# A hybrid decoder layer on one core: the scores of all four pairs of heads in one block, and the last two pairs taken out one gate tile sooner

## The chip, the core and the metric

The kernel runs on one core of a Trainium2 chip. Its engines are TensorE (PE in the profile, with its weight loads PEld), VectorE (DVE), ScalarE (ACT), GpSimd (POOL) and SyncE (SP), which here only issues transfers. Each engine works through its own queue in order and waits for the others by semaphores. The metric is device time in microseconds (us) of one execution, as the median of several runs.

## The reference, cut to what matters

One layer over 256 tokens of width 1024, all in float32: a norm, an input projection `w_in` into q, k, v (8 heads of 64), a pooling input and two gates of 1024 features; causal attention (all 256 tokens lie in one block, so block selection adds nothing) beside a causal multi-scale pooling; both branches projected, gated, summed and projected out; then a gated FFN with a depthwise convolution.

```python
q = apply_partial_rotary(rmsnorm(heads(q), q_norm_g), pos)
k = apply_partial_rotary(rmsnorm(heads(k), k_norm_g), pos)
attn = moba_attention(q, k, heads(v))          # softmax(q k^T / 8, causal) v, per head
pooled = multiscale_pool_mixer(u_pool, w_pool, pool_scale)
gates = sigmoid(gate_logits + b_gate)
mixed = gates[0] * (attn @ w_branch_attn) + gates[1] * (pooled @ w_branch_pool)
x = x + mixed @ w_out
```

## The kernel before, in words

**Numbers and weights.** Each float32 operand is split into a rounded part (`high`, on ACT, tiles `hi_*`) and the rest (`low`, on DVE, tiles `lo_*`); a product takes three matmuls (`mm3`: hi·hi, hi·lo, lo·hi). Weights come in blocks of 1 MB, numbered in the order in which they are used: 15 and 16 are the last two blocks of the gates (`raw_g`), 17 and 18 `w_branch_pool` (`raw_bp`), 19 and 20 `w_branch_attn` (`raw_ba`), 21 to 24 `w_out` (`raw_o`). There are four raw buffers: block c is loaded once block c-4 has been split (`loads`, called from `next_low`). `ahead()` puts the next pieces of splitting into the queues of ACT and DVE between other work.

**Stages around the change.** After q, k, v and the pooling input come 16 gate tiles of 24 matmuls each (`ps_g0` to `ps_g15`, loop over `n`). Between them lie the scores of the attention. The eight heads make four pairs; a pair's two heads use the upper and the lower 64 rows of TensorE. The product of the small projections of pooling, `pool_maps`, comes ahead of gate tile 12. Then come eight tiles of the pool branch (`ps_bp0` to `ps_bp7`); in the midst of them, after tile 4, TensorE multiplies the softmax weights with the values (`values`, `ps_o`). Then come eight tiles of the attention branch (`ps_ba0` to `ps_ba7`), whose moving operand is `heads`, and then `w_out` and the FFN.

**One pair's way.** Scores on TensorE (10 instructions); on DVE the causal mask is added and the row's maximum taken (`sm`, `mx`); on ACT the exponentials, with their sums (`rsum`); on DVE a transposition of 32x32 blocks; on SP a store to memory (`spill`, `home_w`) and four loads (`fill`) that finish the transposition; on TensorE the values. The reciprocals of the sums take a way of their own after the last pair: DVE (`yr`), a store `home_sums`, and two loads into `RS`. `rounded` multiplies the values with `RS` on DVE and rounds on ACT, and `rests` makes the low part of `heads` on DVE.

**What sets the order.** The order is written out: instructions stand in each queue as the Python code calls them, and a last loop ties each engine to it. `later(n, fn)` puts a step n gate tiles (later: n pairs of branch tiles) off. While `paused[0]` is set, `loads` issues nothing of itself; from then on single blocks are let through by `loads(1)` in `turn_weights` (after the last pair's store) and in `fill_late` (after the last fills), until `fill_late` lifts the pause.

**PSUM and SBUF.** `mm` has four single banks, which all tiles of 256 columns use in turn; `ps2` has two pairs of banks. In the kernel before, each pair's scores take one pair of banks, so two pairs are done ahead of gate tile 6 and two ahead of gate tile 10, each time followed by their masks. In SBUF `big` is a tag with two buffers (first q and k, then `sm0` and `y0`), and "qk" and "at" are the places of the split q and k.

Of the kernel before, what the change touches and what calls it, by code (L numbers as in the profile page):

```python
# [7 lines left out]
F32 = mybir.dt.float32  # L8
F32R = mybir.dt.float32r
AF = mybir.ActivationFunctionType  # L10
ALU = mybir.AluOpType
AX = mybir.AxisListType

P = 128
S = 256
NT = S // P
D = 1024
KD = D // P
H = 8
DH = 64  # L20
# [34 lines left out]
FFN_AHEAD = 6  # L55
MAPS = 6
VALUES = 4
GATES = (4, 5, 0, 1, 2, 6, 7, 3)
PLAIN = (4, 5, 6, 7, 8, 9)
HALVED = 2  # L60
# [10 lines left out]
def hybrid_layer_kernel(ctx: ExitStack, tc: tile.TileContext, xq_d, xtok_d, par_d, wkv_d, wpg_d,  # L71
                        wpool_d, wba_d, wbp_d, wout_d, wup_d, wdn_d, out_d):
    nc = tc.nc
# [5 lines left out]
    act = ctx.enter_context(tc.tile_pool(name="act", bufs=1))  # L79
# [3 lines left out]
    ps2 = pairs.enter_context(tc.tile_pool(name="ps2", bufs=2, space=bass.MemoryType.PSUM))  # L83
    tmp = mixer.enter_context(tc.tile_pool(name="tmp", bufs=2))

    def bank(name):
        return mm.tile([P, 512], F32, tag="mm", name=name)
# [57 lines left out]
    for c, (name, src) in enumerate(order):  # L145
        n = CH if name == "q" else src.shape[-1]
# [3 lines left out]
    for c in range(len(order) - 1):  # L150
        if order[c][0] == "dn" and order[c + 1][0] == "up":
            i = next(n for n, p in enumerate(pieces) if p[0] == c)
            pieces[i + 1:i + 4] = [*pieces[i + 2:i + 4], pieces[i + 1]]
    pieces[0:HALVED] = [(0, slice(256 * i, 256 * (i + 1)), i == 0, False) for i in range(2 * HALVED)]
    at = [0, 0]
# [31 lines left out]
    paused = [False]  # L187
# [67 lines left out]
    mask = const.tile([P, 2, P], F32, name="mask")  # L255
# [25 lines left out]
    rows = dram.tile([1, S], F32, name="rows")  # L281
# [61 lines left out]
    def big(name):  # L343
        return tmp.tile([P, 2 * 2 * 3 * P], F32, tag="big", bufs=2, name=name)
# [135 lines left out]
    for b in range(2):  # L480
        w = chunk("p")
        for c in range(2):
            ps = feature_tile(w, c, f"u{b}{c}")
# [15 lines left out]
    qp = act.tile([P, 2, KA, S], F32R, tag="qk", name="qp")  # L499
    kp = act.tile([P, 2, KA, S], F32R, tag="at", name="kp")  # L500
# [18 lines left out]
    def gate(n):  # L519
        return gates[:, n // 2, n % 2, :]  # L520
# [3 lines left out]
    TOK = (slice(0, P), slice(P, 3 * P))  # L524

    whole = mask.rearrange("p a b -> p (a b)")

    turned = []

    def scores(hps):  # L530
        if not turned:
            sms, ys = big("sm0"), big("y0")
            turned.append(ys)
        else:
            sms = turned.pop()
            ys = act.tile([P, 2 * 2 * 3 * P], F32, tag="qk", name="y2")
        pss = []
        for hp in hps:
            pss.append(ps2.tile([P, 2, 512], F32, tag="ps2", name=f"ps_s{hp}"))
            for t, part, keys in ((1, 1, 0), (1, 0, 0), (1, 0, 1), (0, 0, None), (0, 1, 0)):  # L540
                for j in range(2):
                    rows = slice(j * DH, (j + 1) * DH)
                    out = pss[-1][:, j, TOK[t]]
                    if keys is None:
                        out = pss[-1][:, j, :].rearrange("p (a b) -> p a b", b=P)[:, 0:4:3, :]
                    nc.tensor.matmul(out, qp[rows, part, hp, t * P:(t + 1) * P],
                                     kp[rows, :, hp, 0:P] if keys is None else kp[rows, keys, hp, 0:(t + 1) * P],
                                     start=t == part == 1, stop=(t, part, keys) in ((1, 0, 1), (0, 1, 0)),
                                     skip_group_check=True)
        for i, (hp, ps) in enumerate(zip(hps, pss)):  # L550
            on = slice(i * 6 * P, (i + 1) * 6 * P)
            sm = sms[:, on].rearrange("p (j c) -> p j c", j=2)
            mx = tmp.tile([P, 2, 2], F32, tag="mx", name=f"mx{hp}")
            nc.vector.tensor_tensor(sm[:, :, TOK[0]], ps[:, :, 3 * P:4 * P],
                                    mask[:, 1:2, :].to_broadcast([P, 2, P]), ALU.add)
            for j in range(2):
                for t in (1, 0):
                    nc.vector.tensor_tensor_reduce(sm[:, j, TOK[t]], ps[:, j, TOK[t]],
                                                   whole if t else sm[:, j, TOK[0]], 1.0, LOWEST,
                                                   ALU.add, ALU.max, mx[:, t, j:j + 1])  # L560
            nc.vector.scalar_tensor_tensor(mx, mx, -1.0, qs[:, :, 2 * hp:2 * hp + 2], ALU.mult, ALU.mult)
            if i == 0:
                exponentials(hp, sm, mx, ys[:, on], sms[:, on])
            else:
                behind.append((exponentials, hp, sm, mx, ys[:, on], sms[:, on]))
# [16 lines left out]
    RS = []  # L582
# [22 lines left out]
    def fill_late(far):  # L605

        for weights in late:
            fill_weights(*weights)
        loads(1)
        RS.append(act.tile([P, H // 2 * NT * P], F32, tag="qk", name="RS"))  # L610
        for j in range(2):
            src = far.rearrange("(a i) r -> a (i r)", a=4)[None, :, j * S:(j + 1) * S].to_broadcast([DH, 4, S])
            nc.sync.dma_start(out=RS[0][j * DH:(j + 1) * DH, :].rearrange("p (a c) -> p a c", a=4), in_=src)
        paused[0] = False
        loads()

# [10 lines left out]
        return po  # L627

    def weighed(hp):
        return RS[0].rearrange("p (a h t r) -> p h a t r", a=4, t=NT, r=32)[:, hp]  # L630

    def natural(hp):
        return weighed(hp).rearrange("p a t r -> p t a r")
# [43 lines left out]
    for n in range(2 * KD):  # L677
        if n == 1:
            for _ in range(2):
                next_high()  # L680
            for _ in range(2):
                next_low()
        if n in (2, 3):
            part_high("q" if n == 2 else "k")
        if n in (6, 10):
            scores((0, 1) if n == 6 else (2, 3))
            paused[0] = n == 10
        if n == 2 * MAPS:
            pool_maps()
            ahead()  # L690
        b, c = n // 2, n % 2
        if c == 0:
            w = chunk("g")
        ps = feature_tile(w, c, f"g{n}")
        tick()
        ahead(AHEAD if n % 2 else 0)
        for fn, *args in behind + held:
            fn(*args)
        behind.clear()
        held.clear()  # L700
        f = 2 * GATES[b] + c
        if n in PLAIN:
            nc.scalar.activation(gate(f), ps[:, 0:S], AF.Copy)
            plain.append(f)
        else:
            nc.vector.tensor_tensor(gate(f), ps[:, 0:S], R1, ALU.mult)
        if n in (2, 3):
            part_low("q" if n == 2 else "k")
        if n >= 2 * KD - 2:
            sigmoids(3)  # L710
# [10 lines left out]
    for j in range(KD):  # L721
        if j % 4 == 0:
            w = chunk("bp")
        ps = branch("p", poolh, pooll, j, w)
        if j == VALUES:
            pos = [(hps, values(hps)) for hps in ((0, 1), (2, 3))]
        if j in (VALUES, VALUES + 1):
            nc.vector.tensor_tensor(gate(KD + j), ps[:, 0:S], gate(KD + j), ALU.mult)
            for hps, po in pos:
                rounded(hps, po) if j == VALUES else rests(hps)  # L730
        if j % 2 == 1:
# [4 lines left out]
        sigmoids(1)  # L736
        if j not in (VALUES, VALUES + 1):
            nc.vector.tensor_tensor(gate(KD + j), ps[:, 0:S], gate(KD + j), ALU.mult)
# [7 lines left out]
    for j in range(KD):  # L746
        if j % 4 == 0:
            w = chunk("ba")
        ps = branch("a", heads[0], heads[1], j, w)
# [47 lines left out]
    for b in range(4):  # L797
        w = chunk("o")
        ps = [bank(f"ps_out{b}{c}") for c in range(2)]
# [93 lines left out]
    ps = [bank("ps_up1_0")]  # L893
# [6 lines left out]
    for i in range(1, KF):  # L900
        if i > 1:
            w = chunk("up")
            ps = [up_tile(w, 0, i)]
# [101 lines left out]
```

## Time and profile before

| | |
|---|---|
| median of 3 runs | 328.79 us (328.37 to 328.88) |
| the profiled execution's own time | 328.88 us |
| its span, first to last instruction | 327.1 us (1.8 us lie around it) |
| busy, share of the span | PE 322.7 us (99%), PEld 316.1, DVE 259.3 (79%), ACT 201.8 (62%), POOL 71.5 (22%) |
| granted clock of TensorE | 1.0 |
| moved by DMA | 69.72 MB, 213 GB/s on the mean |

A row of the timeline has the start in us from the span's first instruction, the duration, the engine, the line, the operation, what it writes and reads, the shape, and the count of like instructions merged; a bracket gives the idle time of the engine before it and what ended it. Matmuls overlap in the pipe, so the distance of two starts, not the duration, is what one costs. Buffer numbers are left out in the profile's names: `raw_ba` stands for blocks 19 and 20.

### The profile page before, as it was taken

The numbers are of one execution on the slowest core, as the hardware profiler recorded it, in microseconds if no ns is written. First come the engines' busy times: TensorE is split into PE (matmuls) and PEld (weight loads), VectorE is DVE, ScalarE is ACT, GpSimd is POOL, SyncE is SP. The second block draws the span as 40 slices with busy tenths as digits, with TensorE's granted clock in tenths as the row PEclk, the third lists the DMA queues.
The fourth block names the chain that finished last, engine by engine and source line by source line (L and its number), as shares of the span: only waits on it lengthen the run. The fifth ranks groups of instructions, "written<-read, shape, count | busy, mean of one in ns | idle before, by whom it ended". The sixth has DMA issues, their size and how long they took to land.

```text
span 327.1 us, 6769 instructions
## 1 busy us (share of the span) xinstructions
PE 322.7 (99%) x2708; PEld 316.1 (97%) x2708; DVE 259.3 (79%) x447; ACT 201.8 (62%) x329; POOL 71.5 (22%) x89
## 2 busy tenths in 40 slices
PE   8999999999999999999999999999999999999995
PEld 8888899999999999999999999999999999999995
DVE  4839989999988966879997978686868686868834
ACT  5768518675994657669675647474747474746520
POOL 1006690000000151230421221212121212121330
PEclk9999999999999999999999999999999999999999
DMA  7999799947799833635527455464646464643003
GB/s 263 420 415 236 200 373 299 310 141 280 260 284 336 318 128 127 254 137 178 208 100 288 178 208 212 174 217 172 217 169 215 172 219 167 222 164 130 0 2 128
DMA packets 16542, 69.72 MB, mean 213 GB/s; under 512 B 2176, under 2 KB 7040, under 8 KB 9856
## 3 DMA queue, kind: packets, MB, share of 16 engines
q1 hardware_dynamic: 16096, 69.17, 60.1%
q8 instruction: 21, 0.34, 0.4%
q10 hardware_dynamic: 416, 0.13, 0.2%
q14 instruction: 9, 0.07, 0.1%
HBM read 65.61 MB, written 3.69 MB: 212 GB/s over the span
## 4 chain that ended last, share of the span: by engine, by line
PE 99%; DVE 0%; issue 0%
PE ps_up L105 12%; PE ps_up L103 12%; PE ps_up L104 12%; PE ps_d L867 6%; PE ps_d L865 6%; PE ps_d L866 6%; PE ps_g L103 5%; PE ps_g L105 4%; PE ps_g L104 4%; PE ps_q L333 4%; PE ps_k L333 3%; PE ps_v L333 3%; PE ps_out L103 2%; PE ps_out L105 2%; PE ps_out L104 2%; PE ps_warm L248 1%
## 5 line engine op out<-in xcount | busy, mean ns | idle before, releaser
L105 PE MATMUL ps_up<-hhi,lo_up 128*128 128x256 f32 x352 | 97.2, 276 | 0.0
L103 PE MATMUL ps_up<-hhi,hi_up 128*128 128x256 f32 x352 | 97.2, 276 | 0.0
L104 PE MATMUL ps_up<-hlo,hi_up 128*128 128x256 f32 x352 | 97.2, 276 | 0.0
L104 PEld LDWEIGHTS ps_up<-hlo,hi_up 128*128 128x128 f32 x352 | 66.1, 188 | 0.0
L105 PEld LDWEIGHTS ps_up<-hhi,lo_up 128*128 128x128 f32 x352 | 66.1, 188 | 0.0
L103 PEld LDWEIGHTS ps_up<-hhi,hi_up 128*128 128x128 f32 x352 | 66.1, 188 | 0.0
L95 DVE TENSOR_TENSOR lo_up<-raw_up,hi_up 128x1024 fp32r<-128x1024 f32 x44 | 54.7, 1261 | 7.3 <-ACT hi_up L91 7.3
L865 PE MATMUL ps_d<-ah,hi_dn 128*128 128x256 f32 x176 | 48.6, 276 | 0.0
L866 PE MATMUL ps_d<-al,hi_dn 128*128 128x256 f32 x176 | 48.6, 276 | 0.0
L867 PE MATMUL ps_d<-ah,lo_dn 128*128 128x256 f32 x176 | 48.6, 276 | 0.0
L91 ACT ACTIVATE hi_up<-raw_up 128x1024 fp32r<-128x1024 f32 x44 | 44.1, 1046 | 0.0
L847 POOL TENSOR_TENSOR c_v<-c_g,c_v 128x256 f32<-128x256 f32 x22 | 16.3, 739 | 121.4 <-DVE c_v L830 121.4
L91 ACT ACTIVATE ah<-c_v 128x256 fp32r<-128x256 f32 x22 | 9.2, 418 | 45.6 <-POOL c_v L847 45.6
L103 PE MATMUL ps_g<-xhi,hi_g 128*128 128x256 f32 x128 | 35.6, 278 | 0.0
L105 PE MATMUL ps_g<-xhi,lo_g 128*128 128x256 f32 x128 | 35.4, 276 | 0.0
L104 PE MATMUL ps_g<-xlo,hi_g 128*128 128x256 f32 x128 | 35.4, 276 | 0.0
L865 PEld LDWEIGHTS ps_d<-ah,hi_dn 128*128 128x128 f32 x176 | 33.0, 188 | 0.0
L866 PEld LDWEIGHTS ps_d<-al,hi_dn 128*128 128x128 f32 x176 | 33.0, 188 | 0.0
L867 PEld LDWEIGHTS ps_d<-ah,lo_dn 128*128 128x128 f32 x176 | 33.0, 188 | 0.0
L95 DVE TENSOR_TENSOR lo_dn<-raw_dn,hi_dn 128x1024 fp32r<-128x1024 f32 x22 | 27.8, 1263 | 0.4 <-ACT hi_dn L91 0.4
L835 DVE TENSOR_TENSOR u_v<-ps_up,R 128x256 f32<-128x256 f32 x22 | 9.3, 421 | 20.9 <-PE ps_up L105 20.8
L872 POOL TENSOR_TENSOR al<-c_v,ah 128x256 fp32r<-128x256 f32 x22 | 22.0, 1002 | 11.6 <-ACT ah L91 11.6
(197 smaller groups left out, 780.9 us busy)
## 6 DMA issues: line engine op xcount, KB each, us to landing
raw_up<-in_wup SPq DMA_DIRECT2D x22, 1024.0 KB, 4.9
raw_g<-in_wpg SPq DMA_DIRECT2D x8, 1024.0 KB, 8.4
raw_dn<-in_wdn SPq DMA_DIRECT2D x8, 1024.0 KB, 4.9
raw_o<-in_wout SPq DMA_DIRECT2D x4, 1024.0 KB, 10.6
raw_dn<-in_wdn SPq DMA_DIRECT2D x6, 512.0 KB, 4.9
raw_v<-in_wkv SPq DMA_DIRECT2D x2, 1024.0 KB, 15.5
raw_p<-in_wpg SPq DMA_DIRECT2D x2, 1024.0 KB, 13.1
raw_bp<-in_wbp SPq DMA_DIRECT2D x2, 1024.0 KB, 5.4
```

The source lines that it names most:

```text
L91: nc.scalar.activation(hi, src, AF.Copy, scale=scale)
L95: nc.vector.tensor_tensor(lo, src, hi.bitcast(F32), ALU.subtract)
L103: nc.tensor.matmul(out, sh, mh, start=start, stop=False, **kw)
L104: nc.tensor.matmul(out, sh, ml, start=False, stop=False, **kw)
L105: nc.tensor.matmul(out, sl, mh, start=False, stop=stop, **kw)
L333: nc.tensor.matmul(pt[t][:, c:c + wide], sx[:, k, t * P:(t + 1) * P], wx[:, sl], start=k == 0 and c == 0 and sx is xhi and wx is hi, stop= ...
L835: nc.vector.tensor_tensor(u, ps[:, 0:S], R2, ALU.mult)
L847: nc.gpsimd.tensor_tensor(uc[1], g[1], uc[1], ALU.mult)
L865: nc.tensor.matmul(o, hi[:, sl], acch[i], start=first, stop=False, skip_group_check=True)
L866: nc.tensor.matmul(o, hi[:, sl], accl[i], start=False, stop=False, skip_group_check=True)
L867: nc.tensor.matmul(o, lo[:, sl], acch[i], start=False, stop=i == KF - 1, skip_group_check=True)
L872: nc.gpsimd.tensor_tensor(accl[i], act_i, acch[i].bitcast(F32), ALU.subtract)
```

## The change

All four pairs' scores are computed in one block ahead of gate tile 6, in the order 0, 2, 3, 1. Pairs 0 and 1 each take two of the single banks of `mm`; pairs 2 and 3 take the two pairs of banks of `ps2`, and are held there. Pairs 0 and 1 are masked at once, pairs 2 and 3 ahead of gate tile 9 (`LATE`), no more ahead of gate tile 10. The first mask addition of a pair, one instruction over both heads, becomes two, since the heads' banks no longer lie together. `sm` and `y` of the last two pairs lie where the split q and k were, and `RS` takes a `big` buffer. The pause of the loads is set ahead of gate tile 8 (`LATE - 1`), where it was set ahead of gate tile 10.

```diff
+LATE = 9
...
-    def scores(hps):
-        if not turned:
-            sms, ys = big("sm0"), big("y0")
-            turned.append(ys)
+    def score_steps(hp):
+        if hp < 2:
+            ps = [bank(f"ps_s{hp}{j}") for j in range(2)]
         else:
-            sms = turned.pop()
-            ys = act.tile([P, 2 * 2 * 3 * P], F32, tag="qk", name="y2")
+            both = ps2.tile([P, 2, 512], F32, tag="ps2", name=f"ps_s{hp}")
+            ps = [both[:, j, :] for j in range(2)]
...
+    pss = {}
+
+    def scores():
+        for hp in (0, 2, 3, 1):
+            pss[hp] = score_steps(hp)
+
+    def masked(hps):
+        if hps[0] == 0:
+            ys, sms = big("y0"), big("sm0")
+        else:
+            sms, ys = (act.tile([P, 2 * 2 * 3 * P], F32, tag=tag, name=f"{name}2")
+                       for tag, name in (("qk", "sm"), ("at", "y")))
+        for i, hp in enumerate(hps):
+            ps = pss[hp]
...
-            nc.vector.tensor_tensor(sm[:, :, TOK[0]], ps[:, :, 3 * P:4 * P],
-                                    mask[:, 1:2, :].to_broadcast([P, 2, P]), ALU.add)
+            for j in range(2):
+                nc.vector.tensor_tensor(sm[:, j, TOK[0]], ps[j][:, 3 * P:4 * P], mask[:, 1, :], ALU.add)
...
-        RS.append(act.tile([P, H // 2 * NT * P], F32, tag="qk", name="RS"))
+        RS.append(big("RS"))
...
-        if n in (6, 10):
-            scores((0, 1) if n == 6 else (2, 3))
-            paused[0] = n == 10
+        if n == 6:
+            scores()
+        if n in (6, LATE):
+            masked((0, 1) if n == 6 else (2, 3))
+        if n == LATE - 1:
+            paused[0] = True
```

On TensorE, the scores ahead of gate tile 6 stood so before (pairs 0 and 1; `ps_s0` and `ps_s1` are pairs of banks):

```order
L105 MATMUL ps_g5_785<-xhi_83,lo_g10_643 128x256
L546 MATMUL ps_s0_815<-kp_615,qp_614 128x256 x6
L546 MATMUL ps_s0_815<-kp_615,qp_614 128x2x128 x2
L546 MATMUL ps_s0_815<-kp_615,qp_614 128x128 x2
L546 MATMUL ps_s1_826<-kp_615,qp_614 128x256 x6
L546 MATMUL ps_s1_826<-kp_615,qp_614 128x2x128 x2
L546 MATMUL ps_s1_826<-kp_615,qp_614 128x128 x2
L103 MATMUL ps_g6_855<-xhi_83,hi_g11_650 128x256
```

In the changed kernel, on TensorE, the end of pair 0 (single banks `ps_s00`, `ps_s01`), pairs 2 and 3, and the start of pair 1 (`ps_s10`, `ps_s11`) at the same place:

```order
L541 MATMUL ps_s00_813<-kp_615,qp_614 128x128
L541 MATMUL ps_s01_814<-kp_615,qp_614 128x128
L541 MATMUL ps_s2_825<-kp_615,qp_614 128x256 x6
L541 MATMUL ps_s2_825<-kp_615,qp_614 128x2x128 x2
L541 MATMUL ps_s2_825<-kp_615,qp_614 128x128 x2
L541 MATMUL ps_s3_836<-kp_615,qp_614 128x256 x6
L541 MATMUL ps_s3_836<-kp_615,qp_614 128x2x128 x2
L541 MATMUL ps_s3_836<-kp_615,qp_614 128x128 x2
L541 MATMUL ps_s10_847<-kp_615,qp_614 128x256
L541 MATMUL ps_s11_848<-kp_615,qp_614 128x256
```

The 20 score instructions that stood ahead of gate tile 10 now stand here, between pairs 0 and 1; the count of matmuls is the same.

On DVE, the work around the transpositions of the last two pairs (`y2`) and the turned sums (`yr`) before, from the low part of the last pooled group on:

```order
L95 TENSOR_TENSOR pooll_445<-pl3_1008,poolh_444 128x256
L95 TENSOR_TENSOR lo_g15_977<-raw_g15_716,hi_g15_976 128x1024
L706 TENSOR_TENSOR xq_82<-ps_g10_1059,R1_169 128x256
L292 STREAM_TRANSPOSE y2_1018<-y0_814 128x6x4x32
L95 TENSOR_TENSOR lo_g16_1086<-raw_g16_782,hi_g16_1085 128x1024
L292 STREAM_TRANSPOSE y2_1018<-y0_814 128x6x4x32
L592 RECIPROCAL rsum_175<-rsum_175 128x16
L594 STREAM_TRANSPOSE yr_1128<-rsum_175 128x32
```

The same place on DVE in the changed kernel:

```order
L293 STREAM_TRANSPOSE y2_1008<-sm2_1007 128x6x4x32
L96 TENSOR_TENSOR pooll_445<-pl3_1054,poolh_444 128x256
L96 TENSOR_TENSOR lo_g15_1003<-raw_g15_716,hi_g15_1002 128x1024
L293 STREAM_TRANSPOSE y2_1008<-sm2_1007 128x6x4x32
L602 RECIPROCAL rsum_175<-rsum_175 128x16
L604 STREAM_TRANSPOSE yr_1105<-rsum_175 128x32
L719 TENSOR_TENSOR xq_82<-ps_g10_1068,R1_169 128x256
L96 TENSOR_TENSOR lo_g16_1098<-raw_g16_782,hi_g16_1097 128x1024
```

The evacuation of gate tile 10 and one piece of block 16 stood ahead of `yr`, and now stand behind it.

On SP, the transfers from the second block of `w_branch_pool` to the first of `w_out` before:

```order
L135 DMA raw_bp18_980<-in_wbp 128x2048
L296 DMA home_w2_1120<-y2_1018 128x768
L296 DMA home_w3_1125<-y2_1018 128x768
L296 DMA home_sums_1130<-yr_1128 128x32
L135 DMA raw_ba19_1132<-in_wba 128x2048
L304 DMA y0_814<-home_w2_1120 32x4x192 x4
L304 DMA y0_814<-home_w3_1125 32x4x192 x4
L135 DMA raw_ba20_1185<-in_wba 128x2048
L613 DMA RS_1187<-home_sums_1130 64x4x256 x2
L135 DMA raw_o21_1230<-in_wout 128x2048
```

The same transfers on SP in the changed kernel:

```order
L297 DMA home_w2_1094<-y2_1008 128x768
L297 DMA home_w3_1102<-y2_1008 128x768
L297 DMA home_sums_1107<-yr_1105 128x32
L136 DMA raw_bp18_1109<-in_wbp 128x2048
L305 DMA sm2_1007<-home_w2_1094 32x4x192 x4
L305 DMA sm2_1007<-home_w3_1102 32x4x192 x4
L136 DMA raw_ba19_1145<-in_wba 128x2048
L623 DMA RS_1147<-home_sums_1107 64x4x256 x2
L136 DMA raw_ba20_1170<-in_wba 128x2048
L136 DMA raw_o21_1237<-in_wout 128x2048
```

Each of blocks 18, 19 and 20 has moved one place back: 18 from ahead of the stores to where 19 was, 19 to where 20 was, and 20 behind the two loads of `RS`, where 21 was.

More of the change, by code (lines that the diff above doesn't have):

```diff
@@ L526, in hybrid_layer_kernel @@
     whole = mask.rearrange("p a b -> p (a b)")
-    turned = []
-    def scores(hps):
-        if not turned:
-            sms, ys = big("sm0"), big("y0")
-            turned.append(ys)
-        else:
-            sms = turned.pop()
-            ys = act.tile([P, 2 * 2 * 3 * P], F32, tag="qk", name="y2")
[L537 to L550, printed above, removed]
@@ new lines, in score_steps @@
+    def score_steps(hp):
+        if hp < 2:
+            ps = [bank(f"ps_s{hp}{j}") for j in range(2)]
+        else:
+            both = ps2.tile([P, 2, 512], F32, tag="ps2", name=f"ps_s{hp}")
+            ps = [both[:, j, :] for j in range(2)]
+        for t, part, keys in ((1, 1, 0), (1, 0, 0), (1, 0, 1), (0, 0, None), (0, 1, 0)):
+            for j in range(2):
+                rows = slice(j * DH, (j + 1) * DH)
+                out = ps[j][:, TOK[t]]
+                if keys is None:
+                    out = ps[j].rearrange("p (a b) -> p a b", b=P)[:, 0:4:3, :]
+                nc.tensor.matmul(out, qp[rows, part, hp, t * P:(t + 1) * P],
+                                 kp[rows, :, hp, 0:P] if keys is None else kp[rows, keys, hp, 0:(t + 1) * P],
+                                 start=t == part == 1, stop=(t, part, keys) in ((1, 0, 1), (0, 1, 0)),
+                                 skip_group_check=True)
+        return ps
@@ L553, in scores @@
             mx = tmp.tile([P, 2, 2], F32, tag="mx", name=f"mx{hp}")
-            nc.vector.tensor_tensor(sm[:, :, TOK[0]], ps[:, :, 3 * P:4 * P],
-                                    mask[:, 1:2, :].to_broadcast([P, 2, P]), ALU.add)
+            for j in range(2):
+                nc.vector.tensor_tensor(sm[:, j, TOK[0]], ps[j][:, 3 * P:4 * P], mask[:, 1, :], ALU.add)
             for j in range(2):
                 for t in (1, 0):
-                    nc.vector.tensor_tensor_reduce(sm[:, j, TOK[t]], ps[:, j, TOK[t]],
+                    nc.vector.tensor_tensor_reduce(sm[:, j, TOK[t]], ps[j][:, TOK[t]],
                                                    whole if t else sm[:, j, TOK[0]], 1.0, LOWEST,
@@ L609, in fill_late @@
         loads(1)
-        RS.append(act.tile([P, H // 2 * NT * P], F32, tag="qk", name="RS"))
+        RS.append(big("RS"))
         for j in range(2):
             src = far.rearrange("(a i) r -> a (i r)", a=4)[None, :, j * S:(j + 1) * S].to_broadcast([DH, 4, S])
-            nc.sync.dma_start(out=RS[0][j * DH:(j + 1) * DH, :].rearrange("p (a c) -> p a c", a=4), in_=src)
+            nc.sync.dma_start(out=RS[0][j * DH:(j + 1) * DH, 0:H // 2 * S].rearrange("p (a c) -> p a c", a=4), in_=src)
         paused[0] = False
@@ L629, in weighed @@
     def weighed(hp):
-        return RS[0].rearrange("p (a h t r) -> p h a t r", a=4, t=NT, r=32)[:, hp]
+        return RS[0][:, 0:H // 2 * S].rearrange("p (a h t r) -> p h a t r", a=4, t=NT, r=32)[:, hp]
     def natural(hp):
```

## The prediction, made before the changed kernel ran

> **What bounds the kernel now.** I read first the engines' busy shares and then what TensorE waits for; these rows are of the page and of the view of waits.
>
> ```profile
> span 327.1 us, 6769 instructions
> PE 322.7 (99%) x2708; PEld 316.1 (97%) x2708; DVE 259.3 (79%) x447; ACT 201.8 (62%) x329; POOL 71.5 (22%) x89
> PE ps_warm L248 <- DVE ones L216: 1.1, 1, 1.1
> ```
>
> TensorE is busy for 99% of the span, and its only wait is 1.1 us at the start. So there are two ways in which the change can count: it makes TensorE's own stream of instructions shorter, or it makes TensorE wait where it did not. The sum is made against the profiled execution, 328.88 us, which lies 0.09 above the median of 328.79.
>
> **The score blocks on TensorE.** The third view is TensorE's timeline at the first block. A score instruction uses 64 rows; the rows that start at 65.93 and 66.35 are the second step of the first pair and the first step of the second pair, read from narrower windows. The last row is the second block.
>
> ```profile
> 65.50 0.28 PE L105 MATMUL ps_g<-xhi,lo_g 128*128 128x256 f32 x1
> 65.71 1.39 PE L546 MATMUL ps_s<-kp,qp 64*128 64x256 f32 x20
> 65.93 0.58 PE L546 MATMUL ps_s<-kp,qp 64*128 64x256 f32 x8
> 66.35 0.75 PE L546 MATMUL ps_s<-kp,qp 64*128 64x256 f32 x10
> 67.03 0.38 PE L103 MATMUL ps_g<-xhi,hi_g 128*128 128x256 f32 x1
> 67.25 0.28 PE L104 MATMUL ps_g<-xlo,hi_g 128*128 128x256 f32 x1
> 65.39 0.28 PE L104 MATMUL ps_g<-xlo,hi_g 128*128 128x256 f32 x1
> 78.18 1.39 PE L546 MATMUL ps_s<-kp,qp 64*128 64x256 f32 x20
> ```
>
> Gate matmuls start 0.11 apart (65.39 to 65.50). From 65.50 to 67.25 it is 1.75 instead of 0.23, so a block of two pairs costs 1.52, and two such blocks (both rows say 1.39) cost 3.05. A pair inside a block, with gate matmuls on neither side, takes less: four of its five steps are 66.35 - 65.93 = 0.42, and the other step lies between 0.11 and the 0.22 that it took after the switch (65.71 to 65.93). That makes 0.53 to 0.64, and I take the middle, 0.59. One block of four costs 1.52 + 2 x 0.59 = 2.70. **The merge is worth 0.34 us** (0.24 to 0.46). This is all that TensorE's stream can gain.
>
> **The single banks, costed at nothing.** Gate tile 6 now needs the bank of `ps_s00`, and pair 1 needs the banks of gate tiles 4 and 5.
>
> ```profile
> 66.56 0.42 DVE L554 TENSOR_TENSOR sm<-ps_s,mask 128x256 f32<-128x256 f32 x1
> 66.90 0.41 DVE L558 CUSTOM_DVE_ANT_0 sm<-ps_s,mask 128x256 f32<-128x256 f32 x1
> 67.24 0.29 DVE L558 CUSTOM_DVE_ANT_0 sm<-ps_s,sm 128x128 f32<-128x128 f32 x1
> 67.45 0.42 DVE L558 CUSTOM_DVE_ANT_0 sm<-ps_s,mask 128x256 f32<-128x256 f32 x1
> 66.23 0.38 ACT L703 ACTIVATE xq<-ps_g 128x256 f32<-128x256 f32 x1
> ```
>
> DVE's starts are 0.34 apart at 256 columns and 0.21 at 128. Two half additions instead of one whole cost 2 x 0.21 - 0.34 = 0.08 a pair, taking the reduction's pace for the addition's. The bank of `ps_s00` is free at 66.56 + 0.42 + 0.34 + 0.29 = 67.61; TensorE wants it at 67.03 + 2 x 0.59 = 68.21. Gate tile 5 is out at 66.61; pair 1 wants its bank at 65.71 + 0.64 + 2 x 0.59 = 67.5. The covers are 0.6 and 0.9 us.
>
> **What moves on DVE ahead of `home_sums`.** DVE waits for nothing from here to 97.4, so its times are sums.
>
> ```profile
> 83.88 0.42 DVE L706 TENSOR_TENSOR xq<-ps_g,R 128x256 f32<-128x256 f32 x1
> 84.22 0.97 DVE L292 STREAM_TRANSPOSE y<-y 128x768 f32<-128x768 f32 x1
> 85.11 1.18 DVE L95 TENSOR_TENSOR lo_g<-raw_g,hi_g 128x1024 fp32r<-128x1024 f32 x1
> 86.28 0.98 DVE L292 STREAM_TRANSPOSE y<-y 128x768 f32<-128x768 f32 x1
> ```
>
> The evacuation of gate tile 10 (0.34) and a piece of block 16 (1.17) leave the queue ahead of the turned sums; the split additions put in 4 x 0.08. So the sums leave 1.51 - 0.32 = 1.19 us sooner, if ACT's exponentials keep up; if they don't, sooner by less, down to zero.
>
> **The queue of transfers, where the change costs.** SP issues in order. These are its rows before; `y<-home_w` are the eight fills, and the two `raw_ba` are blocks 19 and 20.
>
> ```profile
> 81.97 0.38 SPq L135 DMA_DIRECT2D raw_bp<-in_wbp  x1
> 87.70 1.24 SPq L296 DMA_DIRECT2D home_sums<-yr  x1
> 89.06 0.34 SPq L135 DMA_DIRECT2D raw_ba<-in_wba  x1
> 90.41 4.30 SPq L304 DMA_DIRECT2D y<-home_w  x8
> 94.91 0.35 SPq L135 DMA_DIRECT2D raw_ba<-in_wba  x1
> 95.60 1.33 SPq L613 DMA_DIRECT2D RS<-home_sums  x2
> 97.03 1.02 SPq L135 DMA_DIRECT2D raw_o<-in_wout  x2
> ```
>
> How long each took to land, from the transfers of single stretches (the last column; the rows are block 19, block 20 and block 21), with the steady loads of the FFN behind:
>
> ```profile
> raw_ba<-in_wba SPq DMA_DIRECT2D x1, 1024.0 KB, 5.3
> raw_ba<-in_wba SPq DMA_DIRECT2D x1, 1024.0 KB, 6.2
> raw_o<-in_wout SPq DMA_DIRECT2D x1, 1024.0 KB, 10.1
> raw_up<-in_wup SPq DMA_DIRECT2D x22, 1024.0 KB, 4.9
> ```
>
> A load behind fills and `RS` waits for them: block 21, behind block 20 and `RS`, took 10.1 us, and a load alone takes 4.9. With the pause set two tiles sooner, blocks 18, 19, 20 take the places of 19, 20, 21, with the same neighbours and sizes, so I move those rows by 1.19. Block 18 is issued at 89.06 - 1.19 = 87.9 (81.97 before) and lands at 93.2. Block 19 lands at 94.91 + 6.2 - 1.19 = 99.9 (94.4 before). **Block 20 lands at 97.03 + 10.1 - 1.19 = 105.9** (94.91 + 6.2 = 101.1 before), 4.8 us later.
>
> Blocks 18 and 19 have room, nearly: block 19 holds DVE ahead of the evacuation of branch tile 0 until about 102.3, and TensorE wants that bank at about 102.4. Block 20 has none: it is what ACT waits for already.
>
> ```profile
> 101.17 1.06 ACT L91 ACTIVATE hi_ba<-raw_ba 128x1024 fp32r<-128x1024 f32 x1 [2.37 <-DMA raw_ba<-in_wba]
> 102.27 1.23 DVE L95 TENSOR_TENSOR lo_ba<-raw_ba,hi_ba 128x1024 fp32r<-128x1024 f32 x1 [0.73 <-ACT hi_ba L91]
> 104.74 0.42 DVE L728 TENSOR_TENSOR xq<-ps_bp,xq 128x256 f32<-128x256 f32 x1
> 105.76 0.76 DVE L644 TENSOR_TENSOR RS<-ps_o,RS 128x256 f32<-128x256 f32 x2 [0.60 <-PE ps_o L625]
> 107.06 0.75 DVE L644 TENSOR_TENSOR RS<-ps_o,RS 128x256 f32<-128x256 f32 x2 [0.55 <-PE ps_o L625]
> 107.74 1.22 DVE L95 TENSOR_TENSOR lo_ba<-raw_ba,hi_ba 128x1024 fp32r<-128x1024 f32 x1
> 109.54 1.42 DVE L95 TENSOR_TENSOR heads<-RS,heads 128x256 fp32r<-128x256 f32 x4
> 111.26 0.28 PE L104 MATMUL ps_ba<-heads,hi_ba 128*128 128x256 f32 x1
> ```
>
> Behind the high part of block 20 on ACT, and behind its low part on DVE, stands the whole way to `heads`. ACT starts 0.1 after the landing and takes 1.06: the low part starts at 107.1, not 102.27. The L728 step follows 2.47 behind, at 109.5; the four products with `RS`, 0.34 apart, no longer wait for TensorE and run from 109.9 to 111.2; the second low part starts then, 3.5 later than before, and the low parts of `heads` 1.8 behind it, at 113.0, not 109.54. The first is out about 0.4 later, at 113.4. TensorE's second matmul of the attention branch needs it, and started at 111.26. DVE's and TensorE's idle room (0.60 + 0.55, and 1.3) is used up, and **TensorE stands 2.2 us behind its old times**. The 0.34 of the merge, and any wait of branch tiles 4 and 6 for banks, lie ahead of this wait and vanish in it. The FFN, with PE at 99%, gives nothing back. Sum: 328.88 + 2.2 = 331.1 us.
>
> The ends: block 20 at the 4.9 of a lone load, issued at 97.03 - 1.19 = 95.8, lands at 100.7 and nobody waits: 328.5. With the sums no sooner than before it lands at 107.1, and all is 1.2 worse: 332.3. I take 105.9, since the row of block 21 has the same transfers ahead of it.
>
> The Trainium skill (DMA: Bandwidth & Descriptors, Anatomy of one DMA) has a fit of 2.0 us plus bytes by 436e3 per us for one transfer, of another issuing path; that is an estimate of 4.4 us for 1 MB, by which block 20 would land at about 100.2 and the sum would be 328.5, as in the first rival below. The trace is near it for lone loads (4.9) and far from it here (10.1). The same page (Queues, rings and completion order) says that each DMA engine takes a queue's descriptors in ring order, which is how the 10.1 reads.
>
> **The rivals.** First, *not slower*: the late block does no harm, since the fills and `RS` drain faster than in the old row. For it speaks the 4.9; against it, the 6.2 and 10.1 of the same stretch. It gives 328.88 - 0.34 = 328.5 and decides if block 20 lands before about 103.4; up to 104.3 the time is still within 0.2%. Second, *the banks*: DVE comes later to pair 0 than at 66.56, and gate tile 6 waits. Over 0.6 us late it would cost the excess, 0.2 to 0.5 us, so 328.5 to 329.0 where block 20 is early; where block 20 is late, this too vanishes. Third, *more*: blocks 18 and 19 hold ACT and DVE as well, so that the last products and the loads of `w_out` also come late; 332.3 to 333.5.
>
> **How the numbers follow.** About 0.2% (0.66 us) is what a measurement can tell here. Late block 20 at 330.2 to 332.3: 0.60. More than that: 0.08. Partly late, 329.4 to 330.2: 0.06. Not slower, with or without the banks: 0.26, of which 0.05 is faster by over 0.2%, for which the switches would have to cost twice what the rows say. So faster 0.05, same 0.21, slower 0.74. The range has to reach to the other sign to hold 8 in 10: 328.4 to 332.3; the likeliest case's own range is 330.2 to 332.3.
>
> **What would show it.** Right: one block of 40 score instructions of about 2.6 us; `raw_ba` landing in the second place after about 10 us; ACT idle for some 3 us ahead of its third `hi_ba`; and among TensorE's waits a new one of about 2 us for `heads` by DVE. Wrong: TensorE's waits still 1.1 us in all, or a landing of block 20 ahead of 103.4.

## The result, and the profile after

The changed kernel takes 331.88 us (median of 6 runs, 331.51 to 332.71); the kernel before, run beside it, 328.71 (6 runs, 328.36 to 329.14). The ratio is 1.010, with a 95% interval from 1.0086 to 1.0114: slower by 3.2 us, where the prediction said 2.2 (331.1, in a range from 328.4 to 332.3). The profiled execution took 332.71, the slowest of the six, and its span is 330.9, against 327.1 before.

TensorE's waits beside the one of 1.1 us at the start (tile and line, what released it: us in total, times, longest):

```profile
PE ps_ba L105 <- DVE heads L96: 1.7, 1, 1.7
PE ps_bp L104 <- DVE xq L751: 0.5, 1, 0.5
```

Before, there was only the wait at the start; now there are a wait of 1.7 us for `heads` and one of 0.5 us in the pooled branch just ahead of it. They make 2.2 us; shorter waits do not stand in this view, so the whole loss is read from the starts of matmuls, below. The merged block of scores, on TensorE's timeline (start, duration):

```profile
65.89 0.28 PE L106 MATMUL ps_g<-xhi,lo_g 128*128 128x256 f32 x1
66.09 2.57 PE L541 MATMUL ps_s<-kp,qp 64*128 64x256 f32 x40
68.59 0.38 PE L104 MATMUL ps_g<-xhi,hi_g 128*128 128x256 f32 x1
68.81 0.28 PE L105 MATMUL ps_g<-xlo,hi_g 128*128 128x256 f32 x1
```

From 65.89 to 68.81 it is 2.92, less 0.23 for two gate matmuls: the block of four costs 2.69. SP's queue (start, duration of the issues):

```profile
86.79 0.38 SPq L297 DMA_DIRECT2D home_sums<-yr  x1
87.23 0.46 SPq L136 DMA_DIRECT2D raw_bp<-in_wbp  x1
87.88 6.02 SPq L305 DMA_DIRECT2D sm<-home_w  x8
93.95 0.43 SPq L136 DMA_DIRECT2D raw_ba<-in_wba  x1
94.43 1.38 SPq L623 DMA_DIRECT2D RS<-home_sums  x2
95.90 0.56 SPq L136 DMA_DIRECT2D raw_ba<-in_wba  x1
```

The landings (the last column, us after the issue) of block 18, block 19 and block 20, each from the transfers of a single short window:

```profile
raw_bp<-in_wbp SPq DMA_DIRECT2D x1, 1024.0 KB, 6.4
...
raw_ba<-in_wba SPq DMA_DIRECT2D x1, 1024.0 KB, 5.2
...
raw_ba<-in_wba SPq DMA_DIRECT2D x1, 1024.0 KB, 10.4
```

Block 20, now behind `RS` as well as the fills, is issued at 95.90 and lands 10.4 us later, at 106.3 (101.1 before). What stands behind it, from the timelines of ACT, DVE and TensorE:

```profile
106.36 1.06 ACT L92 ACTIVATE hi_ba<-raw_ba 128x1024 fp32r<-128x1024 f32 x1 [3.46 <-DMA raw_ba<-in_wba]
107.45 1.22 DVE L96 TENSOR_TENSOR lo_ba<-raw_ba,hi_ba 128x1024 fp32r<-128x1024 f32 x1 [3.03 <-ACT hi_ba L92]
110.27 1.40 DVE L654 TENSOR_TENSOR RS<-ps_o,RS 128x256 f32<-128x256 f32 x4
113.39 1.42 DVE L96 TENSOR_TENSOR heads<-RS,heads 128x256 fp32r<-128x256 f32 x4
111.91 0.28 PE L104 MATMUL ps_ba<-heads,hi_ba 128*128 128x256 f32 x1
113.86 0.38 PE L105 MATMUL ps_ba<-heads,hi_ba 128*128 128x256 f32 x1 [1.67 <-DVE heads L96]
```

ACT sits idle for 3.46 us for the load, DVE for 3.03 us for ACT, and TensorE's second matmul of the attention branch starts at 113.86, 2.6 us behind the 111.26 of before.

The traces of the two profiled executions differ by 3.87 us at TensorE's last matmul. Up to the first gate matmul the changed kernel's is 0.44 later. The gate tiles, from the first gate matmul to the first of the pooled branch, take 47.58 us, not 48.06 (0.48 less, about 0.35 of it the score blocks). From there to TensorE's first matmul on `ps_up` it is 50.39, not 46.48 (3.91 more). The rest is 179.72 us in both. So everything that the change costs lies in one stretch, and this stretch is the measure in what follows: the first matmul on `ps_bp` to the first on `ps_up`.

### The profile page after: what moved, and what is told of

Same layout as the page of the kernel before. It is cut to its first block, busy times and chain, and to the rows that moved or that the text cites. A ratio compares the mean times of both kernels' runs of the same rounds, so it can differ in the third digit from the quotient of the medians.

```text
span 330.9 us, 6770 instructions
## 1 busy us (share of the span) xinstructions
PE 324.2 (98%) x2708; PEld 316.8 (96%) x2708; DVE 259.3 (78%) x451; ACT 202.0 (61%) x329; POOL 71.4 (22%) x89
## 4 chain that ended last, share of the span: by engine, by line
PE 80%; DVE 10%; DMA 5%; POOL 1%; issue 1%; ACT 1%; SPq 0%; DVEq 0%; POOLq 0%
PE ps_up L105 12%; PE ps_up L104 12%; PE ps_up L106 12%; PE ps_d L879 6%; PE ps_d L878 6%; PE ps_d L880 6%; PE ps_q L334 4%; DMA raw_o<-in_wout 3%; PE ps_k L334 3%; PE ps_v L334 3%; PE ps_out L105 2%; PE ps_out L106 2%; PE ps_out L104 2%; DMA raw_bp<-in_wbp 2%; PE ps_g L104 2%; PE ps_g L106 2%
## 5 line engine op out<-in xcount | busy, mean ns | idle before, releaser
L880 PE MATMUL ps_d<-ah,lo_dn 128*128 128x256 f32 x176 | 48.6, 276 | 0.0
L878 PE MATMUL ps_d<-ah,hi_dn 128*128 128x256 f32 x176 | 48.6, 276 | 0.0
L879 PE MATMUL ps_d<-al,hi_dn 128*128 128x256 f32 x176 | 48.6, 276 | 0.0
```

What stands on the lines that cost most here:

```text
L878: nc.tensor.matmul(o, hi[:, sl], acch[i], start=first, stop=False, skip_group_check=True)
L879: nc.tensor.matmul(o, hi[:, sl], accl[i], start=False, stop=False, skip_group_check=True)
L880: nc.tensor.matmul(o, lo[:, sl], acch[i], start=False, stop=i == KF - 1, skip_group_check=True)
```

## The experiments

The stretch and block 20's landing (counted from the first matmul on `ps_bp`), read from the trace of every kernel that ran; the names are those of the experiments below. `ps_bp`, `ps_ba` and `ps_out` are the three parts of the stretch. Each row is one profiled execution.

```
kernel                  block 20 stands    lands    stretch   ps_bp   ps_ba   ps_out
before                  ahead of RS         3.8      46.5     13.8    10.9    21.8
two more switches       ahead of RS         3.0      46.5     13.8    10.9    21.8
code fetch moved out    ahead of RS         4.8      46.5     13.8    10.9    21.8
merge alone, again      ahead of RS         5.7      47.1     13.8    10.9    22.4
code fetch moved in     ahead of RS         6.1      47.5     13.8    11.0    22.6
old order kept          ahead of RS         6.2      48.4     13.8    11.9    22.7
merge and freed DVE     ahead of RS         6.6      47.1     13.8    11.5    21.8
sums behind 20          ahead of RS         7.2      48.6     13.8    12.0    22.7
merge alone             ahead of RS         7.3      48.8     13.8    12.2    22.7
freed DVE               behind RS           8.5      49.0     14.2    13.1    21.8
after                   behind RS           9.0      50.4     14.7    13.0    22.7
old pause sooner        behind RS           9.4      50.8     15.2    12.9    22.7
pause back              behind RS           9.7      51.1     15.3    13.0    22.7
```

The kernel before spread from 328.3 to 332.3 us on the chips of these experiments, so differences of less than 1 us are read from the traces, not from medians.

**The pause alone, in the kernel before.**

```diff
         if n in (6, 10):
             scores((0, 1) if n == 6 else (2, 3))
-            paused[0] = n == 10
+        if n == 8:
+            paused[0] = True
```

> The kernel before with one part of the change alone: the pause of the loads is set ahead of gate tile 8 instead of 10. Scores, masks and banks as before. Theory: the loads alone make the loss. The sums leave at 87.7 as before, so block 20 lands at about 107.1; low parts of heads start 4.7 us later than 109.5, TensorE waits about 3.4 for them and about 0.9 more at the output projection, as in the changed kernel; time 332.2 to 333.6. Rival A (the scores' new place makes the loss): time 328.5 to 329.0.

It took 333.17 us (6 runs, 332.63 to 333.6), ratio 1.0112 (1.0087 to 1.0138). Nothing else of the change is in it. SP's queue:

```profile
95.60 1.33 SPq L613 DMA_DIRECT2D RS<-home_sums  x2
97.03 0.55 SPq L135 DMA_DIRECT2D raw_ba<-in_wba  x1
```

The landing of block 20:

```profile
raw_ba<-in_wba SPq DMA_DIRECT2D x1, 1024.0 KB, 9.7
```

TensorE's waits:

```profile
PE ps_ba L104 <- DVE heads L95: 1.5, 1, 1.5
PE ps_bp L103 <- DVE xq L739: 1.1, 1, 1.1
```

The same place in the queue, nearly the same landing (106.7, and 106.3 in the changed kernel) and waits in the same two branches. They are shared out differently: the wait in the pooled branch is for an evacuation that stands on DVE behind the low part of block 19, which landed at 101.1 here (99.2 in the changed kernel). The 1.5 us for `heads` is less than I had expected; ahead of the last projection the two branches lose 3.3 us together. So the place of the pause is enough to make the loss; scores, banks and buffers are not needed for it.

**The pause put back, in the changed kernel.**

```diff
-        if n == LATE - 1:
+        if n == 10:
             paused[0] = True
```

> The changed kernel with the pause of the loads set ahead of gate tile 10 again, as in the kernel before; scores and masks stay as changed. Block 18 goes back ahead of the stores and block 19 to the place after the sums, but block 20 still stands behind the loads of RS. Theory (only the landing of block 20 counts, and it does harm from about 103.5 us on): blocks 19 and 20 land one 1 MB load (about 2.6 us) sooner than in the changed kernel, 20 at about 103.6 instead of 106.3; TensorE waits 0 to 0.5 us beside the start's 1.1; time 328.4 to 328.8, that is, about as before or up to 0.3 faster. Rival A (the merged block or the single banks cost, whatever the loads do): TensorE's waits and the time stay at 331 to 332. Rival B (block 20 behind RS is what costs, whenever it lands): time still 330 or more.

It took 333.15 us (6 runs, 331.98 to 334.0), ratio 1.0112 (1.0081 to 1.0143): a clear miss. The landings of block 18, block 19 and block 20:

```profile
raw_bp<-in_wbp SPq DMA_DIRECT2D x1, 1024.0 KB, 7.7
...
raw_ba<-in_wba SPq DMA_DIRECT2D x1, 1024.0 KB, 9.5
...
raw_ba<-in_wba SPq DMA_DIRECT2D x1, 1024.0 KB, 7.3
```

SP's queue, with the eight fills first:

```profile
91.19 5.71 SPq L305 DMA_DIRECT2D sm<-home_w  x8
96.95 2.17 SPq L623 DMA_DIRECT2D RS<-home_sums  x2
99.22 0.55 SPq L136 DMA_DIRECT2D raw_ba<-in_wba  x1
```

Block 18 is ahead of the stores again and block 19 ahead of the fills, but they took 7.7 and 9.5 us (6.1 and 5.3 before), the last fill came out only when block 19 had landed, and `RS` was still ahead of block 20, which so landed at 106.5, as late as in the changed kernel. That the fill waited for this landing stands among SP's waits:

```profile
SPq L305 <- DMA raw_ba<-in_wba: 1.9, 1, 1.9
```

All thirteen traces have it so: the eighth fill is issued within 0.03 us after the landing of the 1 MB block ahead of the fills (block 19, or block 18 where the pause is set sooner). In the traces the transfers use eight semaphores in turn, and the eighth fill waits on the one of that block. So a late block there also delays the issue of all that stands behind the fills. The time went with the landing, as the theory has it; what I had wrong was the landing (I had expected 103.6). Two things stay to be told apart: the place of `RS`, and why blocks 18 and 19 took so long.

**`RS` behind block 20, in the changed kernel.**

```diff
         loads(1)
+        paused[0] = False
+        later(1, fill_sums, far)
+
+    def fill_sums(far):
         RS.append(big("RS"))
...
-        paused[0] = False
         loads()
```

> The changed kernel with one thing moved: the two loads of RS are issued one gate tile later, so block 20 stands ahead of them. Pause as changed, so blocks 18 and 19 are as late as in the changed kernel. Theory (the landing of block 20): it lands about 2.6 us behind block 19, at about 101.8 instead of 106.3, RS at about 103 and 105.3, just in time for 105.4; TensorE waits 0 to 0.5 us beside the start's; time 328.4 to 328.9. Rival C (all three late blocks hold ACT and DVE, and their delays add up): DVE still late at heads, time 330 to 331.5.

It took 329.52 us (12 runs, 329.09 to 331.01), ratio 1.0006 (0.9985 to 1.0027). SP's queue:

```profile
93.59 0.91 SPq L136 DMA_DIRECT2D raw_ba<-in_wba  x2
94.55 1.35 SPq L627 DMA_DIRECT2D RS<-home_sums  x2
```

The landing of block 20, and then what is left of TensorE's wait:

```profile
raw_ba<-in_wba SPq DMA_DIRECT2D x1, 1024.0 KB, 9.7
```

```profile
PE ps_ba L105 <- DVE heads L96: 0.7, 1, 0.7
```

Blocks 18 and 19 land as late as in the changed kernel (93.2 and 98.8); only block 20 has moved, ahead of `RS`, and lands at 103.8. By the median most of the loss is gone; the profiled execution, at 330.33 one of the slower ones, still has a stretch of 48.6. The merge alone (below), with block 20 landing at 7.3 and not 7.2 us into the stretch, has 48.8, although its blocks 18 and 19 landed 3.7 and 2.4 us sooner. So it is block 20 that decides, not 18 and 19. That the landing is 103.8 and not 101.8, as I had expected, is the load of block 19 in front of it: two blocks issued 0.5 us apart land 5.0 apart.

**Two more switches, in the kernel before**: three gate matmuls between the two pairs of each block of scores.

```diff
         for hp in hps:
+            if pss:
+                between()
...
+            scores((0, 1) if n == 6 else (2, 3), lambda: gate_part(w, part_ps, range(1)))
```

> The kernel before with two more switches between score and gate matmuls: in each of the two blocks the first three matmuls of the following gate tile are put between the two pairs. Only TensorE's order changes. Theory (the merge is worth 0.34 us for one switch there and back, 0.24 to 0.46): each more costs the same, so time 0.68 above the kernel before (0.48 to 0.92), about 329.4. Rival (a switch costs little and a pair in the midst of a block costs as much as the first): less than 0.3 above.

329.33 us (12 runs), ratio 0.9999 (0.998 to 1.0019), against a kernel before that spread from 328.31 to 331.46 beside it: the time cannot tell 0.7 us here. The trace can; TensorE's timeline at the second block's first pair:

```profile
77.80 0.28 PE L105 MATMUL ps_g<-xhi,lo_g 128*128 128x256 f32 x1
78.01 0.80 PE L548 MATMUL ps_s<-kp,qp 64*128 64x256 f32 x10
78.74 0.38 PE L103 MATMUL ps_g<-xhi,hi_g 128*128 128x256 f32 x1
78.96 0.28 PE L104 MATMUL ps_g<-xlo,hi_g 128*128 128x256 f32 x1
```

From 77.80 to 78.96, less 0.23, a pair by itself costs 0.93. Two of them cost 0.34 more than the 1.52 of a block of two, which is the price of one switch there and back, and the prediction had 0.34. The gate tiles as a whole took 48.61 us, 0.55 more than before, where two such switches make 0.68.

**The merge alone**, run twice: last pairs and pause where they stood before.

```diff
-LATE = 9
+LATE = 10
...
-        if n == LATE - 1:
+        if n == LATE:
```

> The changed kernel with the last two pairs masked ahead of gate tile 10 and the pause of the loads set there (LATE = 10), as before the change: what is left of the change is the one block of scores, the single banks and the buffers; SP's order of transfers is the one of before. By the theory (the late block 20 makes the whole loss): block 20 lands at about 101, TensorE waits for heads by nothing, and the time is that of before less the merge's 0.34, 0.1% faster, within what can be told (ratio 0.998 to 1.001). Rival (banks or buffers cost something by themselves): slower than before by 0.3 us or more, with a wait of TensorE for a bank near 66 to 69 us.

> The merge alone a second time (the changed kernel with the last pairs and the pause where they stood before), since its first twelve runs lay in two groups, eight from 327.92 to 328.93 and four from 330.59 to 330.95, and the one profile is of the upper group, with block 18 landing 6.75 us after its issue, block 19 after 7.29 and block 20 at 104.5. Theory (the merge is worth 0.34 and the upper group is late loads, the same wait as in the changed kernel): where the profile is of the lower group, block 20 lands before 103.4 and TensorE has no wait for heads, at 328.2 to 328.5; where it is of the upper group, block 20 lands at about 104.5 again and TensorE waits 0.8 us for heads. Rival (the upper group has nothing to do with the loads): block 20 lands as late in the one as in the other, or a run above 330 has it at about 101.

The first time 328.52 us (12 runs, 327.92 to 330.95), ratio 0.9998 (0.9967 to 1.0029); the second 329.17 (12 runs, 328.19 to 330.06), ratio 1.0006 (0.9986 to 1.0026). No gain is shown, and the two groups of the first time did not come back as groups. In the second profile the gate tiles are 0.48 shorter than before and the stretch is 0.6 longer. Block 20 landed 7.3 us into the stretch in the profile of 330.95 us and 5.7 in that of 328.93; the second has no wait for `heads`, and both follow the table. The profile of 330.95 also shows the rival of the banks at work. The block of scores on TensorE, then nine of pair 1's ten instructions from a narrower window, and in the same profile ACT's evacuation of gate tile 5 and DVE's first step on pair 0:

```profile
65.43 3.02 PE L541 MATMUL ps_s<-kp,qp 64*128 64x256 f32 x40
67.66 0.80 PE L541 MATMUL ps_s<-kp,qp 64*128 64x256 f32 x9
67.23 0.37 ACT L716 ACTIVATE xq<-ps_g 128x256 f32<-128x256 f32 x1
67.29 0.48 DVE L565 TENSOR_TENSOR sm<-ps_s,mask 128x128 f32<-128x128 f32 x2
```

The same two steps of ACT and DVE in the profile of the second time:

```profile
65.68 0.39 ACT L716 ACTIVATE xq<-ps_g 128x256 f32<-128x256 f32 x1
66.42 0.49 DVE L565 TENSOR_TENSOR sm<-ps_s,mask 128x128 f32<-128x128 f32 x2 [0.54 <-PE ps_s L541]
```

Both engines came later to the banks. ACT came to gate tile 5's bank 1.55 us later and was done with it at 67.60; pair 1 needs it, and nine of its ten instructions start only then. DVE came to pair 0 0.87 us later. The block of scores took 3.02, not 2.57, and the gate tiles took 48.09, not 47.58: about 0.5 us, more than the merge brings. Most of it is the wait for ACT, for which the prediction had a cover of 0.9 us.

**The old order of transfers, with the last pairs sooner**: pause back and `RS` behind block 20, both edits from above.

> The changed kernel with the pause set ahead of gate tile 10 and the two loads of RS one tile later, behind block 20: the last pairs leave sooner, but SP's order of transfers is the one of before. It stands against the run in which the pause alone was put back, where block 20 stood behind RS and landed at 106.5. By the theory: block 20 is issued at about 96.9, or at 94.5 if blocks 18 and 19 do not come late this time, and lands at 101 to 103.4, so that the loss is gone: 0.3 faster to 0.3 us slower than before. Rival (the last pairs taken out sooner cost time by themselves, by the stores of their values against block 18): slower than before by over 1 us although block 20 stands ahead of RS, with block 18 landing at 90 again and block 19 at 96.6.

329.5 us (12 runs, 328.72 to 331.51), ratio 1.0019 (0.9995 to 1.0043). Block 18 took 7.5 us and block 19 9.8 us again; block 20, no longer behind `RS`, landed at 102.6 (6.2 into the stretch). Against the pause put back, with only the place of `RS` between them, the stretch is 2.7 us shorter (48.4 and 51.1). The upper end of what I had expected is passed a little. One reason is that `RS`, now last, landed at 107.2, and DVE's products waited for it:

```profile
107.36 1.42 DVE L657 TENSOR_TENSOR RS<-ps_o,RS 128x256 f32<-128x256 f32 x4 [0.69 <-DMA RS<-home_sums]
```

The other is the low parts that DVE is late with at the last projection (below). So the place behind block 20 has a price too, where the loads come late.

**DVE freed between the attention branch's tiles**, in the changed kernel: one piece of `w_out`'s conversion moved behind the last tile.

```diff
-        if j in (1, 3):
+        if j == 1:
             ahead()
...
     low(ml[:, KD - 1, :], mh[:, KD - 1, :], gate(KD - 1))
     ahead()
+    ahead()
```

> The changed kernel with one piece of w_out's conversion taken out of the attention branch's fourth tile and put behind its last: on DVE 1.13 us less stands between the evacuations and the low parts that the last projection waits for. Theory on what the prediction left out: TensorE's loss of 2.9 us in the branches grows to 3.85 at the projection because DVE's queue is 3.85 behind there and nothing in its loop of four engines gives this back; with the piece moved, TensorE's matmuls of ps_out start without the waits of 0.9 us in all, and the time is 0.6 to 0.9 us below the changed kernel's (3.0 to 2.2 above before). Rival (the waits at the projection are for the last pieces of w_out, late by the transfers): the waits stay or grow, and the time is the changed kernel's or above.

330.91 us (9 runs, 330.75 to 331.94), ratio 1.0065 (1.0044 to 1.0087), 2.0 above before, where the changed kernel stood 3.2 above. It is a little better than expected. DVE's timeline at the evacuations of the attention branch's third and fourth tiles, first in the kernel before, with the piece of `w_out` between them:

```profile
116.06 0.41 DVE L753 TENSOR_TENSOR xq<-ps_ba,xq 128x256 f32<-128x256 f32 x1
117.64 1.22 DVE L95 TENSOR_TENSOR lo_o<-raw_o,hi_o 128x1024 fp32r<-128x1024 f32 x1
118.78 0.42 DVE L753 TENSOR_TENSOR xq<-ps_ba,xq 128x256 f32<-128x256 f32 x1
```

The same in the changed kernel:

```profile
119.91 0.41 DVE L766 TENSOR_TENSOR xq<-ps_ba,xq 128x256 f32<-128x256 f32 x1
121.48 1.22 DVE L96 TENSOR_TENSOR lo_o<-raw_o,hi_o 128x1024 fp32r<-128x1024 f32 x1
122.62 0.42 DVE L766 TENSOR_TENSOR xq<-ps_ba,xq 128x256 f32<-128x256 f32 x1
```

And in this kernel:

```profile
118.85 0.41 DVE L766 TENSOR_TENSOR xq<-ps_ba,xq 128x256 f32<-128x256 f32 x1
120.42 0.42 DVE L766 TENSOR_TENSOR xq<-ps_ba,xq 128x256 f32<-128x256 f32 x1
```

Before and after run alike, 3.85 us apart, through the whole chain. In this kernel the fourth evacuation follows 1.57 us behind the third, not 2.71, and the `ps_out` part of the stretch is back at 21.8 from 22.7. So the 0.94 us lost at the last projection is DVE's lag, not late pieces of `w_out`. Block 20 also landed 0.5 us sooner into the stretch here, so the step of the median from 3.2 to 2.0 above before is not DVE's alone.

**The merge alone with DVE freed**, both edits from above.

> The merge alone, with the piece of w_out's conversion moved out of the attention branch's fourth tile as in the run that freed DVE there. By the theories so far: where the loads come in time the time is the merge's own, 328.2 to 328.5 (0.3 to 0.6 below before); where block 20 comes at 104.5 the waits at the last projection are gone and the time is 329.6 to 330.0, not 330.6 to 330.95. Rival (the piece moved to the end makes w_out's blocks late for the last projection): a wait of TensorE there, and 0.5 us or more above the merge alone in the runs with early loads.

328.97 us (12 runs, 327.9 to 332.53), ratio 1.0013 (0.999 to 1.0036). The waits at the last projection are gone (21.8) with block 20 landing 6.6 into the stretch, but the time is not below before. No version here beats the kernel before by what can be measured.

**The code fetch.** A packet of 16 KB of code (the profile calls its queue's kind `instruction`), 1.0 to 2.1 us on one of the DMA engines, falls among block 18's packets (at 82.8 to 83.8 us) in the five profiles with the merged scores and block 18 ahead of the stores, in which blocks 18 and 19 are late; before it falls at 87.6, half a microsecond ahead of block 18's landing. Two kernels move it by splitting matmuls of the projections into halves: the kernel before with 42 of k's split, and the merge alone with 48 of k's and 42 of v's. The first of the two edits:

```diff
-            wide = 256 if name == "q" and k < HALVED else 512
+            wide = 256 if k < {"q": HALVED, "k": 7, "v": 0}[name] else 512
```

> The kernel before, with 42 of the 48 matmuls of the k projection split into two of half the columns: the same columns and the same work, and 42 more matmuls (with their weight loads) in TensorE's code ahead of the scores. It tests why blocks 18 and 19 came late (7.3 to 7.7 us and 7.7 to 9.8, where the kernel before has 6.1 and 5.3) in all the runs with the merged scores in which block 18 stands ahead of the stores: there a code fetch of 16 KB, about 1 us on one of the 16 DMA engines, falls at 82.8 to 83.8, among block 18's packets, and in the kernel before at 87.6. The fetches are 14.3 us apart, and a split pair moves them ahead by about 0.11 us, so 42 of them by 4.7, to 82.9. Theory (the fetch holds one engine of the block back): block 18 lands 7 us or more after its issue, block 19 at 95.8 to 96.6, block 20 at 102 to 104.5; the time 0 to 1.5 us above before. Rival (the merged kernels' buffers or the order of something else does it): block 18 takes 4.9 to 6.2, block 19 lands at about 94.4, block 20 at 101, whatever the fetch; the time is that of before.

> The merge alone (last pairs and pause where they stood before), with all 48 matmuls of the k projection and 42 of the v projection split into halves: 90 more matmuls ahead of the scores, at about 0.11 us each 10.2 us of TensorE's code sooner, so that the fetches of code fall at about 73 and 87.3 (83.1 and 97.5 in the profile of the merge alone), as in the kernel before. Theory (the fetch among block 18's packets makes blocks 18 to 20 late): block 18 lands 4.9 to 6.2 us after its issue, block 19 at 94 to 95, block 20 ahead of 102, nothing waits for heads, and the times lie in one group at 328.2 to 328.6, 0.1 to 0.2% below before. Rival: block 18 takes 6.6 to 7.5 us again, block 20 lands at 102.4 to 104.5, and the times spread up to 330 or 331 as before.

Moved in: 329.88 us (11 runs), ratio 1.0031 (1.0011 to 1.0051), of which the split itself is 0.6 (the k projection took 11.23 us, not 10.65). Moved out: 330.18 (12 runs, 329.26 to 333.02), ratio 1.0045 (1.0022 to 1.0067), with 1.2 us of splitting in it (the k and v projections). Landings of blocks 18 and 19 with the fetch moved in:

```profile
raw_bp<-in_wbp SPq DMA_DIRECT2D x1, 1024.0 KB, 7.8
raw_ba<-in_wba SPq DMA_DIRECT2D x1, 1024.0 KB, 8.4
```

And with it moved out:

```profile
raw_bp<-in_wbp SPq DMA_DIRECT2D x1, 1024.0 KB, 6.8
raw_ba<-in_wba SPq DMA_DIRECT2D x1, 1024.0 KB, 7.0
```

The first is as the theory has it in the landings, though the fetch came at 80.1, among the fills ahead of block 18, not at 82.9. In the second the fetch came at 89.1, 1.4 us ahead of block 18's landing, and block 18 still took 6.8 us, not 4.9 to 6.2; block 20 landed at 102.7, and TensorE did not wait for it. In the kernel with two more switches a fetch fell at 85.7, also ahead of block 18's landing (86.4), and block 18 took 4.9, the least of all. So a fetch early in block 18's time goes with late blocks, but moving it did not bring back the old landings. Why blocks 18 and 19 take from 4.9 to 7.8 and from 5.3 to 9.8 us behind the same neighbours stays open.

## Why the prediction was right, point by point

- *The merge, 0.34.* The block of four cost 2.69 (2.70 predicted), and a switch 0.34 where two were added. Right, and it does not show in the time: about 0.5 us, more than the gain, can be lost again at the banks.
- *The single banks at nothing.* Right in the changed kernel's profile (the block has no wait, and DVE waited 0.94 us for TensorE there). The covers were real, and thin: in one execution of the merge alone ACT used up the 0.9 us of gate tile 5's bank. The rival had looked to DVE and the other cover.
- *DVE, 1.19 us sooner.* The turned sums' store was issued at 86.79, 0.91 sooner, with this execution 0.44 later at the first gate matmul.
- *The queue.* Blocks 18, 19 and 20 were predicted to land at 93.2, 99.9 and 105.9, and landed at 93.6, 99.2 and 106.3. The steps moved from the old rows held within 0.7 us. The Trainium skill's fit for a lone transfer (DMA: Bandwidth & Descriptors, Anatomy of one DMA; an estimate of 4.4 us for 1 MB) does not hold for block 20, which took 10.4; its ring order (Queues, rings and completion order) agrees with the run in which `RS` changed places with block 20 (landing at 103.8, not 106.3).
- *The way to `heads`.* Low part predicted at 107.1 and measured at 107.45; products from 109.9, measured 110.27; low parts of `heads` 113.0, measured 113.39; TensorE 2.2 behind, measured 2.6.
- *Nothing behind it.* This is the step that failed: I put the carry from the branches to the end at nothing. DVE's queue was 3.85 us behind, more than TensorE, and its chain of evacuation, gate, high and low part for the last projection kept that lag. TensorE, 2.6 us behind at `heads`, lost 0.33 more in the attention branch, was 2.93 behind at its first matmul on `ps_out`, waited for DVE there, and lost another 0.94. With DVE freed the 0.94 is gone, and the median is 2.0 above before, not 3.2. So the term that I put at nothing is 0.9 to 1.3 us in these traces, which covers the 0.8 between 331.1 and 331.88.
- *The break-even at 103.4* (6.1 us into the stretch) was too late for the same reason: at 5.7 the stretch is 0.6 longer already, at 4.8 it is not. From 7.3 to 9.0 each us of landing costs 0.98.
- *The rivals.* Not slower: refuted, since block 20 lands behind the point. More: blocks 18 and 19 did land late, but TensorE's wait of 0.5 us in the pooled branch is not their doing: the evacuation that it waited for stood on DVE behind block 20's low part of 107.45. In the run of the pause alone, where block 19 landed at 101.1, it is block 19 that costs TensorE 1.1 us there. The median stays below the 332.3 to 333.5 of this rival, though one execution, the profiled one at 332.71, lies in it.

## What to carry to other kernels

A switch that holds back loads moves every load behind it in the queue: before moving it, write down the queue row by row, find the load that an engine already waits for, and price the new place by the old tenant of that place, not by a lone transfer. Then follow the lag on each engine to the next place where they meet: TensorE's wait at the first place is not the whole cost when another engine stands further behind and its chain has no room to catch up. A gain of a third of a microsecond is not worth covers of less than a microsecond on shared banks.

## What the runs showed that I had not expected

A block of 1 MB took from 4.9 us (block 18 with two more switches) to 7.8 (with the code fetch moved in) in kernels with the same transfers around it, and the next one from 5.3 to 9.8. The DMA queues carry code too: packets of 16 KB, 0.9 to 2.1 us each, some 8 to 18 us apart in the gate tiles, at moments that shift with the code ahead of them. Whether these packets are the cause is not shown.
